# A 1-core network of eight stages: weight splits ahead of use are pinned to ScalarE's program order, and their stores are issued from ScalarE's DMA queue

## The chip, the cores and the metric

The kernel runs on one core of a Trainium2 chip. The metric is the device time of one execution in microseconds. Names used below: TensorE (PE) multiplies, VectorE (DVE) and ScalarE (ACT) work elementwise, GpSimd (POOL) helps them, SyncE (SP) issues DMAs. Each engine runs its own instructions strictly in the order in which they stand.

## What is computed

The reference takes x of 512 rows by 1024 columns in float32 through two blocks of a network. The first block is four residual layers (mixer_a, mixer_b, mixer_c, mixer_a), the second is two layers of a mixer and a gated feed-forward part. Nearly all the work is products of activations with weights. The two kinds that matter here, shortened:

```
def mixer_c(h, w_in, w_grp, scale, w_out):
    proj = h @ w_in                       # 4 groups of xc, then z
    pooled = stack([causal_mean(xc[:, :, g], w) for g, w in enumerate((2, 4, 8, 16))])
    mixed = einsum('bsgc,gcd->bsgd', pooled - xc, w_grp) * scale
    return (mixed * silu(z)) @ w_out

def swiglu(h, w_gate, w_up, w_down):
    return (silu(h @ w_gate) * (h @ w_up)) @ w_down

# first block:  x = x + mixer_a | mixer_b | mixer_c | mixer_a (rms_norm(x))
# second block: x = x + rms_norm(even_mixer | swiglu | odd_mixer | swiglu (rms_norm(x)))
```

## The kernel before

The stages run one after the other and are called a0, b, c, a1 (first block), m0, f0, m1, f1 (second block; m are the mixers, f the feed-forward parts).

**Products in three parts.** A float32 value is held as the sum of a high part (rounded by a Copy on ScalarE) and a low part (value minus high part, a subtraction on VectorE). Each product is three matmuls: high by high, high by low, low by high. A panel of weights (128 x 1024) against 512 rows of activations is therefore 8 x 3 = 24 matmuls of 128x512. `gemm_T` does one panel.

**Weights, the ordinary way.** `wchunk` fetches the raw panel `wr` by a DMA on SP (line 254, in `fetch`), makes `wh` on ScalarE (line 320) and `wl` on VectorE. Each of the three lives in pool `pw` with three buffers, so the preparation can lead TensorE by about two panels. Activations are split likewise into `xh`/`xl`, `mh`/`ml`, `yh`/`yl`.

**Weights, the other way.** The weights of m0, f0's first panels, m1 and f1's first panels are split earlier, in stages with spare time on ScalarE and VectorE, and put back in DRAM as `preh` and `prel`. Their panels are later loaded already split (lines 316, 317, 357 and 358). The generator `presplit` (lines 283 to 311) does this. One step of it loads a raw piece `pr` (line 300, on SP), issues the stores of the piece before (lines 289 and 290), and at its next turn makes `ph` (line 304, ScalarE) and `pl` (VectorE). `pr` has one buffer, `ph` and `pl` have two each. `gemm_T` and its sibling `gemm_tok` give the generator one turn per product (`tick`). The call says how large the pieces are, at every how many turns a piece is made, and how many pieces: 1024 columns, every third, 18 pieces in stage c; 512 columns, every second, in a1; up to 1024 columns, every second, in f0, from its third pair of panels on, beside `ssm_tables`, which builds tables of powers for m1 on VectorE (tiles `E`, `eu`, `btx`). There are 70 pieces: 46 for m0 and f0, and 24 for m1 and f1.

**What sets the order.** A scheduler places the instructions on each engine from the program and from its own model of times, and may hoist an instruction ahead of where the program has it, as early as its operands and buffers allow. An instruction wrapped in `tc.keep_in_program_order` keeps its place among the others of its engine as the program has it. In the kernel before, TensorE and VectorE have such stretches (the class `Ordered`, line 206); ScalarE has none. In the built program of before, the pieces do not stand where the turns of the generator are: all 46 pieces of m0 and f0 stand within stage c, about one ahead of each panel's `wh`, and the 24 of f0 stand in about half of that stage.

**Stage c.** Two halves, each with two pooling groups and an output product. A group has four panels of `c_wx` (each followed by running sums in tiles `pad` and `last`, on VectorE and GpSimd, and the split `mh`/`ml`), four of `c_wz` (then `z` through Silu, line 924), and four panels of 512 columns of `c_wg` against `mh`/`ml`, whose results times `z` are split into `yh`/`yl`. Eight panels of `c_wo` against `yh`/`yl` end the half. At the first of these panels the row norm is turned into a scale: `sc` (VectorE, then line 498 on GpSimd), `t` (a diagonal, VectorE), and a small product `a` of `t` with `ones` on TensorE, which is pinned in TensorE's order ahead of the second half of that panel.

Of the kernel before, what the change touches and what calls it, by code (L numbers as in the profile page):

```python
# [179 lines left out]
def build(nc, tc, A, out, stages=("a0", "b", "c", "a1", "m0", "f0", "m1", "f1")):  # L180
# [6 lines left out]
    AF = mybir.ActivationFunctionType  # L187
# [3 lines left out]
    V, S, G, PE = nc.vector, nc.scalar, nc.gpsimd, nc.tensor  # L191
# [25 lines left out]
    def tl(pool, shape, tag, dt=F32, **kw):  # L217
        uid[0] += 1
        return pool.tile(list(shape), dt, tag=tag, name=f"{tag}_{uid[0]}", **kw)

    with ctx:
# [26 lines left out]
        def f32(t):  # L248
            return t.bitcast(F32)
# [33 lines left out]
        def presplit(pool, cap, every, count):  # L283

            made = []

            def store():
                h, l, wh, wl = made.pop(0)
                nc.sync.dma_start(h, f32(wh))
                nc.sync.dma_start(l, f32(wl))  # L290
            while todo and count:
                w, o = todo.pop(0)
                n = min(cap, w.n - o)
                if o + n < w.n:
                    todo.insert(0, (w, o + n))
                count -= 1
                e = slice(o, o + n)
                wr = tl(pool, (P, cap), "pr")[:, :n]
                wh, wl = (tl(pool, (P, cap), "p" + a, F32R, bufs=2)[:, :n] for a in "hl")
                nc.sync.dma_start(wr, w.src[:, e])  # L300
                if made:
                    store()
                yield
                S.activation(wh, wr, AF.Copy)
                V.tensor_tensor(wl, wr, f32(wh), op=SUB)
                made.append((w.h[:, e], w.l[:, e], wh, wl))
                for _ in range(every - 1):
                    yield
            if made:
                store()  # L310
# [249 lines left out]
        def layer_a(j, nxt):  # L560
            with ExitStack() as c:
# [10 lines left out]
                if todo:  # L572
                    tasks.append(presplit(newpool(c, "pre"), 512, 2, 99))
# [304 lines left out]
        def layer_c(nxt):  # L878
            with ExitStack() as c:
# [9 lines left out]
                if "m0" in stages:  # L889
                    todo.extend((w, 0) for w in m0_weights() + (ffn_first(0) or []))  # L890
                    tasks.append(presplit(newpool(c, "pre"), 1024, 3, 18 if "a1" in stages else 99))
# [782 lines left out]
        def layer_f(l, nxt):  # L1674
            with ExitStack() as c:
# [7 lines left out]
                for part, n in enumerate(FFN_SPLIT):  # L1683
                    Y = []
                    for i in range(i0, i0 + n):
                        if l == 0 and i == 2 and "m1" in stages:
                            todo.extend((w, 0) for w in m1_weights() + (ffn_first(1) or []))
                            tasks.append(presplit(newpool(c, "pre"), 1024, 2, 99))
                            tasks.append(ssm_tables(ptab, Y[-1][0]))
                        pg = first.pop(0) if first else gemm_T(A[f"f{l}_wg"][i], X)  # L1690
                        pu = first.pop(0) if first else gemm_T(A[f"f{l}_wu"][i], X)
                        z = tmp()
                        V.tensor_tensor(z, pg, sb, op=MUL)
                        S.activation(z, z, AF.Silu)
                        V.tensor_tensor(z, z, pu, op=MUL)
                        Y.append(split(py, "y", z))
                    i0 += n
                    if part == len(FFN_SPLIT) - 1:
                        drain()
                        sandwich_end(A[f"f{l}_wd{part}"], Y, O, False, 9 + 2 * l, m1_first() if l == 0 else None, sc)  # L1700
                        break
                    for m in range(KD):
                        ps = gemm_T(A[f"f{l}_wd{part}"][m], Y)
                        if part == 0:
                            V.tensor_copy(O[m], ps)
                        else:
                            V.tensor_tensor(O[m], O[m], ps, op=ADD)
# [43 lines left out]
```

## Time and profile before

| | us |
|---|---|
| three runs | 2947.56, 2938.97, 2943.58 |
| median | 2943.58 |
| the profiled execution | 2942.7 |
| its span in the trace | 2940.9 |
| TensorE busy | 2838.7 (97%) |
| VectorE busy | 1618.5 (55%) |
| ScalarE busy | 1033.9 (35%) |
| GpSimd busy | 212.8 (7%) |

The profiled execution moved 385.48 MB by DMA, and TensorE's mean granted clock in it was 0.983 of full speed. In the trace stage c with the pieces for m0 and f0 fills 940 to 1280 us, a1 goes to about 1680 us, and f0's stretch with the pieces for m1 and f1 is 1945 to 2170 us. A row gives the time that an engine sat idle just before a group of instructions and what ended that wait; on an engine that is not the one that bounds the kernel such idle time costs nothing by itself. Ends of matmuls are modelled, so neighbours overlap by a part of their length.

### The profile page before, as it was taken

How to read it: one execution, taken by the hardware profiler on the slowest of the kernel's cores; microseconds unless marked ns; L12 is line 12 of the kernel's file. 1: busy time of each engine (PE TensorE's matmuls, PEld its weight loads, DVE VectorE, ACT ScalarE, POOL GpSimd, SP SyncE). 2: the span in 40 equal slices, each digit the busy share in tenths (PEclk: the TensorE clock that was granted, in tenths of full speed). 3: DMA queues.
4: the chain of work that ended last, by engine and by line, in shares of the span. 5: the costliest groups of instructions: out<-in, count | busy, mean ns of one | idle time of the engine just before them, and what ended most of it. 6: DMA issues, size and time to landing. Idle time of an engine off the chain costs nothing. (4 is left out here: it accounts for less than half of the span.)

```text
span 2940.9 us, 35039 instructions
## 1 busy us (share of the span) xinstructions
PE 2838.7 (97%) x13542; PEld 2332.4 (79%) x13542; DVE 1618.5 (55%) x3092; ACT 1033.9 (35%) x1661; POOL 212.8 (7%) x187
## 2 busy tenths in 40 slices
PE   8999999999999999899999998889999999999998
PEld 7888888888888777678888886677878865888886
DVE  4454654545556564653554587368753577343434
ACT  4322444444444442342222314443332325332222
POOL 2000000000000101220010100120000200200001
PEclk9999999999999999999999999899999999999999
DMA  4222332222223786642222352257862350333222
GB/s 161 93 86 94 128 112 85 90 76 94 72 95 129 245 281 210 207 153 95 92 93 93 120 188 93 83 181 266 294 221 91 133 178 29 115 108 101 93 99 67
DMA packets 127415, 385.48 MB, mean 131 GB/s; under 512 B 16144, under 2 KB 23056, under 8 KB 127248
## 3 DMA queue, kind: packets, MB, share of 16 engines
q1 hardware_dynamic: 127248, 383.25, 38.7%
q8 instruction: 106, 1.74, 0.2%
q14 instruction: 61, 0.50, 0.1%
HBM read 312.94 MB, written 70.25 MB: 130 GB/s over the span
## 5 line engine op out<-in xcount | busy, mean ns | idle before, releaser
L320 ACT ACTIVATE wh<-wr 128x1024 fp32r<-128x1024 f32 (+2 forms) x408 | 420.6, 1032 | 1005.5 <-PE g L205 781.3
L205 PE MATMUL g<-xh,wl 128*128 128x512 f32 (+1 forms) x1720 | 659.9, 384 | 13.0 <-DVE wl L205 9.6
L205 PE MATMUL g<-xl,wh 128*128 128x512 f32 (+1 forms) x1720 | 661.1, 384 | 11.1 <-DVE xl L205 10.9
L205 PE MATMUL g<-xh,wh 128*128 128x512 f32 (+1 forms) x1720 | 664.8, 387 | 5.8 <-DMA wh<-preh 4.8
L205 DVE TENSOR_TENSOR wl<-wr,wh 128x1024 fp32r<-128x1024 f32 (+2 forms) x408 | 507.7, 1245 | 292.3 <-ACT wh L320 287.2
L205 PE MATMUL g<-yh,wh 128*128 128x512 f32 (+1 forms) x1046 | 394.9, 378 | 1.8 <-ACT yh L438 1.1
L205 PE MATMUL g<-yl,wh 128*128 128x512 f32 (+1 forms) x1046 | 391.2, 374 | 1.6 <-DVE yl L205 1.6
L205 PE MATMUL g<-yh,wl 128*128 128x512 f32 (+1 forms) x1046 | 390.2, 373 | 0.6 <-DVE wl L205 0.6
L205 PEld LDWEIGHTS g<-xh,wl 128*128 128x128 f32 x1720 | 326.3, 190 | 81.1 <-DVE wl L205 15.0
L205 PE MATMUL g<-wh,xh 128*128 128x512 f32 (+1 forms) x992 | 381.3, 385 | 7.8 <-ACT wh L320 7.8
L205 PEld LDWEIGHTS g<-xl,wh 128*128 128x128 f32 x1720 | 326.7, 190 | 75.8 <-DVE xl L205 14.9
L205 PEld LDWEIGHTS g<-xh,wh 128*128 128x128 f32 x1720 | 326.9, 190 | 67.9 <-DMA wh<-preh 5.6
L205 PE MATMUL g<-wl,xh 128*128 128x512 f32 (+1 forms) x992 | 376.5, 380 | 0.3 <-DVE wl L205 0.3
L205 PE MATMUL g<-wh,xl 128*128 128x512 f32 (+1 forms) x992 | 375.2, 378 | 0.0
L470 POOL TENSOR_TENSOR acc<-acc,t 128x256 f32<-128x256 f32 (+1 forms) x109 | 119.6, 1097 | 1708.2 <-issue 1418.3
L205 PEld LDWEIGHTS g<-yh,wh 128*128 128x128 f32 x1046 | 197.6, 189 | 39.4 <-ACT wh L320 2.0
L205 PEld LDWEIGHTS g<-yl,wh 128*128 128x128 f32 x1046 | 197.7, 189 | 38.3 <-DVE yl L205 2.3
L205 PEld LDWEIGHTS g<-yh,wl 128*128 128x128 f32 x1046 | 197.6, 189 | 34.8 <-DVE wl L205 1.0
L205 PEld LDWEIGHTS g<-wh,xh 128*128 128x128 f32 x992 | 187.7, 189 | 41.1 <-ACT wh L320 7.8
L205 PEld LDWEIGHTS g<-wh,xl 128*128 128x128 f32 x992 | 187.6, 189 | 34.3
L205 PEld LDWEIGHTS g<-wl,xh 128*128 128x128 f32 x992 | 187.9, 189 | 33.4 <-DVE wl L205 1.0
L205 DVE TENSOR_TENSOR t<-g,sb 128x512 f32<-128x512 f32 x112 | 77.1, 690 | 234.5 <-PE g L205 233.9
(309 smaller groups left out, 2706.4 us busy)
## 6 DMA issues: line engine op xcount, KB each, us to landing
wh<-preh SPq DMA_DIRECT2D x48, 512.0 KB, 3.6
wl<-prel SPq DMA_DIRECT2D x48, 512.0 KB, 4.3
wr<-in_f_wg_dram SPq DMA_DIRECT2D x40, 512.0 KB, 3.5
wr<-in_f_wu_dram SPq DMA_DIRECT2D x40, 512.0 KB, 3.5
preh<-ph SPq DMA_DIRECT2D x39, 512.0 KB, 5.3
prel<-pl SPq DMA_DIRECT2D x39, 512.0 KB, 6.4
wr<-in_a_wv_dram SPq DMA_DIRECT2D x32, 512.0 KB, 3.5
wr<-in_a_wu_dram SPq DMA_DIRECT2D x32, 512.0 KB, 3.5
```

What stands on the lines that cost most here:

```text
L205: r = f(*a, **k)
L320: S.activation(wh[:, :n], wr[:, :n], AF.Copy)
L470: G.tensor_tensor(self.acc[:, t], self.acc[:, t], sq[:, t], op=ADD)
```

## The change

Two edits in `presplit`. The two stores of each piece are issued from ScalarE's DMA queue and not from SP's. The Copy that makes `ph` is wrapped in `tc.keep_in_program_order`.

```diff
@@ -286,8 +286,8 @@
             def store():
                 h, l, wh, wl = made.pop(0)
-                nc.sync.dma_start(h, f32(wh))
-                nc.sync.dma_start(l, f32(wl))
+                nc.scalar.dma_start(h, f32(wh))
+                nc.scalar.dma_start(l, f32(wl))
...
@@ -301,7 +301,7 @@
                 yield
-                S.activation(wh, wr, AF.Copy)
+                tc.keep_in_program_order(S.activation(wh, wr, AF.Copy))
                 V.tensor_tensor(wl, wr, f32(wh), op=SUB)
```

The built programs show what this moves. ScalarE has 1611 rows for 1471 before (140 stores more), SP 735 for 875; TensorE's order is almost untouched. Of the 46 pieces for m0 and f0, 18 now stand in stage c, one at every third panel, and 28 in a1, at every second product; the 24 of f0 stand at every second panel over most of that stage.

ScalarE in the second group of stage c's first half, at the end of its `c_wx` panels and through its `c_wz` panels (`wh` are panels, `ph` pieces, `mh` the split of the pooled differences):

```order
 L320 ACTIVATE wh_9294<-wr_9296 128x1024
-L304 ACTIVATE ph_11419<-pr_11418 128x512
 L924 ACTIVATE z_9221<-z_9221 128x512
 L320 ACTIVATE wh_9334<-wr_9336 128x512
-L304 ACTIVATE ph_11506<-pr_11505 128x512
+L304 ACTIVATE ph_9326<-pr_9325 128x1024
 L924 ACTIVATE z_9257<-z_9257 128x512
-L304 ACTIVATE ph_11593<-pr_11592 128x512
+L289 DMA preh_1476_7900<-ph_9326 128x1024
+L290 DMA prel_1477_7901<-pl_9327 128x1024
 L320 ACTIVATE wh_9360<-wr_9362 128x512
```

Where three pieces stood within four panels, one stands, right behind a `wh`, with its two stores behind it on the same engine.

VectorE at the opening of stage c, ahead of the norm scale `sc` (`wl` are low parts of panels, `pl` of pieces):

```order
 L205 SCALAR_TENSOR_TENSOR xl_7732<-x_7518,gains_82,xh_7731 128x512
-L205 TENSOR_TENSOR wl_7810<-wr_7811,wh_7809 128x1024
-L205 TENSOR_TENSOR pl_8569<-pr_8567,ph_8568 128x1024
 L205 TENSOR_TENSOR wl_7980<-wr_7981,wh_7979 128x1024
 L205 TENSOR_TENSOR wl_8027<-wr_8028,wh_8026 128x1024
-L205 TENSOR_TENSOR pl_8657<-pr_8655,ph_8656 128x1024
+L205 TENSOR_TENSOR pl_8012<-pr_8010,ph_8011 128x1024
 L205 TENSOR_SCALAR sc_7828<-a_7829 128x4
 L205 TENSOR_SCALAR t_7836<-ident_106,sc_7828 128x128 x4
```

The piece right ahead of `sc` is now the first of the stage and not the seventh or eighth, and the one ahead of it is gone.

VectorE in f0, where the tables of powers are built (`E` and `eu` are steps of a table, `o` a copy of an output product):

```order
-L205 MEMSET E_17398 128x1 x2
+L205 COPY o_15110<-g_16306 128x512
 L205 TENSOR_SCALAR eu_17401<-E_17398,s_3082_15387 128x1
 L205 TENSOR_SCALAR eu_17404<-E_17398,s_3083_15389 128x1
+L205 TENSOR_TENSOR wl_16441<-wr_16442,wh_16440 128x1024
 L205 SCALAR_TENSOR_TENSOR E_17398<-E_17398,s_3083_15389,eu_17401 128x1
```

This table now stands ahead of panel `wl_16441`, which stood well ahead of it before: the tables move forward past panels, and four of the eight fall within ten panels.

## Rows read from the trace of the kernel before

**Rows 1.** Windows of four stretches: length; busy us (instructions) per engine; clock; DMA share; GB/s.

```profile
940.00:1280.00 340.00, 314.27 (x1314) 250.91 (x1313) 204.83 (x283) 131.34 (x176) 48.88 (x32) 0.96 0.71 232
1280.00:1680.00 400.00, 399.74 (x1836) 332.87 (x1835) 192.60 (x226) 118.69 (x162) 35.16 (x23) 1.00 0.30 99
1945.00:2170.00 225.00, 212.93 (x947) 173.76 (x946) 176.87 (x564) 84.68 (x108) 1.90 (x3) 0.98 0.83 281
2170.00:2300.00 130.00, 130.00 (x577) 107.52 (x576) 53.17 (x68) 36.12 (x47) 3.54 (x3) 1.00 0.31 99
```

**Rows 2.** Lines of TensorE, 940 to 1280: count, busy, mean ns, idle before, releaser.

```profile
L205 PE MATMUL g<-xh,wl 128*128 128x512 f32 x256 | 101.8, 398 | 6.0 <-DVE wl L205 6.0
...
L205 PE MATMUL g<-yh,wh 128*128 128x512 f32 x112 | 44.8, 400 | 1.8 <-ACT yh L438 1.1 <-ACT wh L320 0.7
...
L205 PE MATMUL g<-mh,wh 128*128 128x512 f32 x64 | 27.7, 432 | 7.6 <-ACT wh L320 7.6
L205 PE MATMUL g<-mh,wl 128*128 128x512 f32 x64 | 27.5, 430 | 2.6 <-DVE wl L205 2.4
...
L205 PE MATMUL a<-t,ones 128*128 128x128 f32 x8 | 2.1, 441 | 5.5 <-DVE t L205 5.5
```

**Rows 3.** Timeline of ScalarE in the wg panels: start, length, instruction, idle before.

```profile
1191.46 0.63 ACT L304 ACTIVATE ph<-pr 128x512 fp32r<-128x512 f32 x1 [3.40 <-DMA pr<-in_m_wo_dram]
...
1196.77 0.63 ACT L304 ACTIVATE ph<-pr 128x512 fp32r<-128x512 f32 x1 [4.16 <-issue]
1197.31 0.61 ACT L320 ACTIVATE wh<-wr 128x512 fp32r<-128x512 f32 x1
```

**Rows 4.** Lines of ScalarE, line 304: 940 to 1270, then 1945 to 2160.

```profile
L304 ACT ACTIVATE ph<-pr 128x512 fp32r<-128x512 f32 (+1 forms) x46 | 36.7, 798 | 131.8 <-issue 45.7 <-DMA pr<-in_m_wo_dram 31.9 <-DMA pr<-in_m_wqk_dram 21.4
...
L304 ACT ACTIVATE ph<-pr 128x1024 fp32r<-128x1024 f32 (+2 forms) x24 | 24.6, 1024 | 78.0 <-DMA pr<-in_m_wo_dram 15.0 <-DMA pr<-in_m_win_dram 9.7 <-DMA pr<-in_m_wq_dram 9.1
```

**Rows 5.** Timeline of VectorE at the norm scale of stage c, 984 to 994.

```profile
984.85 2.35 DVE L205 TENSOR_TENSOR wl<-wr,wh 128x1024 fp32r<-128x1024 f32 x2
991.43 1.23 DVE L205 TENSOR_TENSOR pl<-pr,ph 128x1024 fp32r<-128x1024 f32 x1 [4.23 <-ACT ph L304]
992.58 0.15 DVE L205 TENSOR_SCALAR sc<-a 128x4 f32<-128x4 f32 x1
993.86 0.88 DVE L205 TENSOR_SCALAR t<-ident,sc 128x128 f32<-128x128 f32 x4 [1.13 <-POOL sc L498]
```

**Rows 6.** Windows of 10 us on TensorE: busy (instructions), clock, DMA share, GB/s.

```profile
990.00:1000.00 10.00, 5.80 (x18) 0.66 0.92 318
1250.00:1260.00 10.00, 9.50 (x37) 0.88 0.46 162
```

**Rows 7.** Lines of TensorE, 1945 to 2170, then of VectorE, 1945 to 2160.

```profile
L205 PE MATMUL g<-xh,wh 128*128 128x512 f32 x230 | 91.1, 396 | 3.5 <-DMA wh<-preh 3.5
...
L205 PE MATMUL g<-xh,wl 128*128 128x512 f32 x229 | 90.6, 396 | 3.6 <-DVE wl L205 3.6
...
L205 PE MATMUL a<-ident,btx 128*128 128x128 f32 x12 | 2.8, 302 | 3.4 <-DVE btx L205 3.4
...
L205 DVE SCALAR_TENSOR_TENSOR E<-E,s,eu 128x1 f32<-128x1 f32 (+5 forms) x144 | 34.6, 271 | 0.3
L205 DVE TENSOR_SCALAR eu<-E,s 128x1 f32<-128x1 f32 (+5 forms) x144 | 30.1, 248 | 1.6
```

**Rows 8.** Timeline of VectorE in the last pooling group, 1234 to 1244.

```profile
1234.62 0.69 DVE L205 SCALAR_TENSOR_TENSOR t<-last,pad 128x512 f32<-128x512 f32 x1 [2.30 <-POOL last L910]
...
1243.21 0.69 DVE L205 SCALAR_TENSOR_TENSOR t<-last,pad 128x512 f32<-128x512 f32 x1 [2.29 <-POOL last L910]
```

**Rows 9.** Tile prel: issue ns min/median/max. Then DMA issues: count, KB, us to landing.

```profile
L290 SPq DMA_DIRECT2D prel<-pl x70: 319/424/1409, 942.7 to 2159.0; - x70
...
preh<-ph SPq DMA_DIRECT2D x39, 512.0 KB, 5.3
prel<-pl SPq DMA_DIRECT2D x39, 512.0 KB, 6.4
```

## The prediction

> **What bounds the kernel now.** The table of busy times is read first: TensorE is busy 2838.7 us of a span of 2940.9, so about 102 us of idle TensorE time and the half-clock time inside the busy part (mean clock 0.983) are all that a change to splits and stores can give back. The windows by stage come next, since an average says nothing on where the 102 us lie [rows 1]. In a1 TensorE is busy 399.74 of 400 us and in the later part of f0 130.00 of 130. That last row gives the price of a matmul at full clock: 130 / 577 = 0.2253 us, so 5.4 us for a panel of 24. In stage c, 1314 matmuls would take 1314 x 0.2253 = 296 us, and they take 340: 44 us are lost, 25.7 as idle time (340 - 314.27), about 13.6 by the clock (4% of 340), the rest at restarts. In f0's stretch with splits 12.1 us are idle and the clock costs 2% of 225 = 4.5.
>
> Third come the releasers of TensorE's idle time in stage c [rows 2]. Nearly all of it is ended by a weight split that came late (`wh` on ScalarE, `wl` on VectorE) or by `t` of the norm scale. None is ended by a DMA. Fourth, why `wh` is late though ScalarE is busy only 131 of 340 us: the timeline of ScalarE [rows 3]. The split `ph` of a piece stands ahead of the panel's `wh`; ScalarE runs in order and sits 3.4 to 4.2 us until the raw piece has come, and only then makes `wh`, at 1197.31. Line 304 takes 131.8 us of idle ScalarE time in this way for 46 pieces, and 78.0 us for the 24 of f0 [rows 4]. The pieces thus go at the pace of their own loop (load, split, store, next load, with one `pr` buffer), and panels that TensorE needs now queue behind pieces that are needed hundreds of microseconds later.
>
> **The change part by part.** The pin puts each piece where the generator's turn is: behind a `wh`, with its raw data fetched a turn or more earlier. A `ph` then costs ScalarE its own length and no wait. The idle times of [rows 2] are taken one by one.
>
> *Norm scale, 5.5 us.* Before `sc`, VectorE makes two `wl` until 987.2, waits 4.2 us for a `ph` and makes its `pl` at 991.43; `sc` follows at 992.58 and `t` at 993.86 [rows 5]. The order now has one piece there, the first of the stage, whose `pr` came long before. Without the wait: 987.2, plus 1.15 for `pl` (991.43 to 992.58), 0.15 for `sc` and 1.13 for GpSimd lets `t` start at 989.6, 4.2 us earlier than at 993.86. So 4.2 of the 5.5 us could go; I take 3.6, since the `pl` may stand a little later behind its `ph`. *The `wg` panels, 7.6 + 2.6 = 10.2 us* [rows 2]: their period is half a panel, 2.7 us, and a `ph` with its wait takes longer than that [rows 3]. Now one piece stands in every three panels and waits for nothing: 9.5 go. *The `yh` panels, 1.8 us, and the small groups* (25.7 - 5.5 - 10.2 - 6.0 - 1.8 = 2.2): 3.5 of 4.0 go, as they too wait for `wh` and `wl`. *The `xh,wl` panels, 6.0 us*: some 3.3 of it lie in the last pooling group, where VectorE's chain waits for GpSimd's running sums every 8.6 us (1234.62 to 1243.21) against 5.4 us for a panel [rows 8]. That chain is the kernel's own and stays. Of the other 2.7, 2.5 go. Together 3.6 + 9.5 + 3.5 + 2.5 = 19 us of idle time.
>
> *The clock.* After long waits the granted clock falls: 0.66 in the 10 us with the norm scale, 0.88 in the last pooling group [rows 6]. Of the 13.6 us in stage c some 3.4 belong to that last group, whose waits stay; 10 go with the waits that go. **Stage c: -29 us**, with -20 as the end where the clock gives little and the other loops stay, and -38 where nearly all of the 44 comes back.
>
> *Pieces moved from c to a1.* 28 splits at 0.63 us on ScalarE and up to 1.2 us on VectorE, their loads and 56 stores now stand in a1. Cover: ScalarE is busy 118.69 of 400 us there, VectorE 192.60, DMA 0.30 [rows 1], and TensorE sees only `wh` and `wl`, which lead by two panels (10.8 us). 18 + 34 us of more work on these two engines leave both under 60%: 0, or +4 where some panel meets a piece with no lead left.
>
> *f0.* Idle before `xh,wl` 3.6 us, before `a<-ident,btx` 3.4, before `xh,wh` 3.5 (the first split panel's own load, in a stretch where DMAs are busy 0.83) [rows 7], and 12.1 - 10.5 = 1.6 in small groups. With half as many pieces per panel and no waits at `ph`: 3.6 + 1.5 + 1.0 + 0.5 = 6.6, plus 2 of the clock's 4.5: -8.6 (from -4 to -13). Against it, the order packs four tables into ten panels. A table costs VectorE (34.6 + 30.1) / 8 = 8.1 us [rows 7]; four of them, ten `wl` and five `pl` at 1.2 us and the copies and products there come to about 55 to 58 us in the 54 us of ten panels: +2 (0 to +4), spread by the lead. **f0: -6.6 us.**
>
> *The stores.* 140 issues leave SP and go to ScalarE. On SP one takes 0.42 us in the median and at most 1.41 [rows 9]. No row shows a store issued by ScalarE, so the price there is bounded: from nothing (a gain is excluded for ScalarE, since it issues no stores now) to the landing of 6.4 us [rows 9] if the issue held the engine until the data is out. I take the SP row's 0.42, since it is the same operation on another queue: 59 us over the whole run, in stretches where ScalarE is idle more than 60% of the time, so 0. The store of `pl` makes ScalarE wait for VectorE; queued behind it are the next `wh` and the next `z` or `yh`. The order puts `pl` right behind a `wl` nearly everywhere, so this wait is a microsecond or two, under the two-panel lead. On SP, panel loads no longer queue behind stores that wait for `ph`, but no TensorE wait in c ends at a load of a raw panel: 0.
>
> The Trainium skill ("DMA: Bandwidth & Descriptors", section "Issuing engines are not separate DMA queues") says that transfers started by different engines share the same 16 DMA engines and that spreading the issues "will only save the time on the sequencer it takes to initiate the DMA". By that rule the queue edit alone gives nothing here, as SP's issue time bounds no panel; the rows above lead to the same 0, and the rule speaks against expecting a gain from the queue, not against the pin.
>
> Sum: -29 + 0 - 6.6 + 0 = -35.6. Against the profiled execution, 2942.7 - 35.6 = **2907 us**. Its time is 0.9 below the median of the runs, which is left aside.
>
> **The rivals.** *Part of the idle time is the kernel's own.* The waits that now end at `wh` would end next at other chains: GpSimd's loop of 8.6 us in the deep pooling groups [rows 8], the norm scale, and VectorE, which is busy 205 of 340 us. Speaking for it: the running-sum loop is there in two groups of four, and VectorE is already the releaser of most of the `xh,wl` and `mh,wl` waits. Against it: the waits at the `wg` panels end at ScalarE, and nothing but the pieces is in front of it. Then c gives 16 and f0 5: 2942.7 - 21 = 2922 us.
>
> *More comes back.* If c runs at full clock but for the last group and f0 loses nothing: 38 + 13 + a few, 2942.7 - 54 = 2889 us.
>
> *The change hardly does what it says.* If the pieces' positions on ScalarE are the new ones but real times let the same loop hold it (a load of `pr` that comes late because its buffer is freed late), the waits move and do not shrink: 2940 us. Against it: two or three panels, 10.8 to 16.2 us, now lie between pieces, and the loop took about 7 us (340 / 46).
>
> *Slower: the stores hold ScalarE.* If each issue on ScalarE occupied it until the data has landed, a pair would take 5.3 + 6.4 = 11.7 us [rows 9]. In f0, with one piece in two panels (10.8 us), ScalarE's other work is (84.68 - 24.6) / 225 x 10.8 = 2.9 us, with the piece's 1.0 it is 3.9 [rows 1, 4], so 15.6 us are needed in 10.8: +4.8 for 24 pieces. In a1 it is 118.69 / 400 x 10.8 = 3.2, plus 0.63 and 11.7, so +4.7 for 28 pieces [rows 1]. Together +115 + 132 = +247: 2907 + 247 = 3154 us. It decides from (10.8 - 3.9) / 2 = 3.4 us per store; the longest issue of a `prel` store on SP took 1.41 [rows 9], which speaks against it.
>
> **How the numbers follow.** Forecast (2890 to 2918): 0.60. Part of the idle time is the kernel's own (2918 to 2930): 0.20. More comes back (under 2890): 0.07. Within 0.3% of the time before, about what a measurement of this kernel can tell from no change (2934 to 2951): 0.06, the case that hardly does what it says. Stores hold ScalarE: 0.07, with smaller holds in it. The range of 2890 to 2930 takes in the forecast and its partial rival, 0.80. Faster is 0.60 + 0.20 + 0.07 = 0.87, same 0.06, slower 0.07.
>
> **What would show it right or wrong.** In the profile of the changed kernel the idle time before line 304 should be near nothing (now 131.8 and 78.0), the waits of TensorE for `wh` in the `mh` groups gone, and the stretch from 940 some 29 us shorter, while a wait of 3 us or so stays in the last pooling group. The clock in the norm scale's 10 us should stand near 0.9. a1 should stay at 400 us with 28 pieces in it. The issues at lines 289 and 290 should read about 0.4 us on ScalarE. It would be wrong if TensorE in a1 showed idle time ended by `wh` or `wl`, if ScalarE's waits before `prel` stores were longer than the two-panel lead, or if f0's table stretch became VectorE's.

## The result and the profile after

The changed kernel takes 2894.24 us in the median (2890.71 to 2899.0, 4 runs) beside 2944.59 us of the kernel before: a ratio of 0.9832, 95% interval 0.9809 to 0.9855. That is faster by 50 us or 1.7%, where 35.6 us were forecast (2907 us); it lies inside the range of 2890 to 2930. The span of the profiled execution is 2888.9 us for 2940.9.

Where the 52 us of span went is read from the start times of the same matmul in both traces. TensorE's matmuls are 13542 in both and stand in nearly the same order, so the n-th of one can be set beside the n-th of the other (n counted from 0; times in us from the start of the span; differences taken before rounding):

| matmul, place | before | after | difference |
|---|---|---|---|
| 4600, ahead of stage c | 915.7 | 916.5 | +0.8 |
| 5000, behind the norm scale of c | 1006.9 | 997.5 | -9.4 |
| 5400, first output product of c | 1107.8 | 1089.0 | -18.8 |
| 5800, where the last pooling group of c begins | 1211.4 | 1179.6 | -31.8 |
| 6400, in a1 | 1356.3 | 1316.7 | -39.7 |
| 8600, in m0 | 1846.0 | 1806.2 | -39.8 |
| 9000, in f0 | 1929.5 | 1889.6 | -39.9 |
| 10000, in f0 behind the tables | 2163.5 | 2112.3 | -51.2 |
| 13400, in f1 | 2907.0 | 2855.1 | -51.8 |

Stage c is 40.4 us shorter (from +0.8 to -39.7), a1 and m0 are unchanged, f0 is 11.4 us shorter, and the rest is under 1 us.

The windows of the same four stretches after the change answer to [rows 1]; the columns are those of that group, and the bounds are moved by the differences above:

```profile
941.00:1241.00 300.00, 297.94 (x1316) 245.12 (x1315) 185.03 (x255) 116.20 (x148) 51.25 (x32) 1.00 0.55 188
1241.00:1641.00 400.00, 399.75 (x1836) 333.12 (x1835) 210.48 (x255) 133.28 (x190) 33.86 (x23) 1.00 0.48 155
1906.00:2119.00 213.00, 208.69 (x945) 172.59 (x946) 172.65 (x560) 80.13 (x104) 1.76 (x2) 1.00 0.74 258
2119.00:2249.00 130.00, 130.00 (x577) 107.55 (x576) 56.90 (x69) 40.25 (x51) 3.81 (x3) 1.00 0.50 164
```

TensorE idles 2.1 of 300 us in stage c, for 25.7 of 340, and the granted clock reads 1.00 in all four. In a1 it is busy 399.75 of 400 us as before, though 28 pieces and their 56 stores now lie there (ScalarE 133.3 us for 118.7, VectorE 210.5 for 192.6, DMA 0.48 for 0.30). In f0 4.3 us are idle, for 12.1.

TensorE's groups in stage c, as in [rows 2] (count, busy, mean ns, idle before, releaser):

```profile
L205 PE MATMUL g<-xh,wl 128*128 128x512 f32 x256 | 99.8, 390 | 0.8 <-DVE wl L205 0.8
...
L205 PE MATMUL g<-mh,wh 128*128 128x512 f32 x64 | 24.9, 389 | 0.0
...
L205 PE MATMUL g<-mh,wl 128*128 128x512 f32 x64 | 24.9, 389 | 0.0
L205 PE MATMUL a<-t,ones 128*128 128x128 f32 x8 | 1.1, 274 | 0.0
```

The 7.6 + 2.6 us at the `wg` panels, the 5.5 at the norm scale and 5.2 of the 6.0 before `xh,wl` are gone. The cause is read on ScalarE, in its group of line 304 over the whole execution, which answers to [rows 4]:

```profile
L304 ACT ACTIVATE ph<-pr 128x1024 fp32r<-128x1024 f32 (+2 forms) x70 | 60.3, 862 | 18.2 <-DMA pr<-in_m_wo_dram 10.4 <-DMA pr<-in_m_wq_dram 2.8 <-DMA pr<-in_s_wg_dram 2.5
```

131.8 + 78.0 us of idle ScalarE time before the pieces have become 18.2. The issues of the store of the low part, now on ScalarE (ns min/median/max), answer to [rows 9]:

```profile
L290 ACTq DMA_DIRECT2D prel<-pl x70: 326/362/363, 985.1 to 2173.1; - x70
```

An issue lasts 0.33 to 0.36 us. The timeline of ScalarE in the third pooling group, the first of the second half, shows one piece from end to end (it is the place of [rows 3] and of the first order listing under "The change"; the text there puts that listing in the first half and in the `c_wx` and `c_wz` panels by mistake: it runs from the last panel of `c_wz` into those of `c_wg`, which are the ones of 512 columns):

```profile
1159.83 0.62 ACT L320 ACTIVATE wh<-wr 128x512 fp32r<-128x512 f32 x1
1160.36 1.04 ACT L304 ACTIVATE ph<-pr 128x1024 fp32r<-128x1024 f32 x1
1161.30 0.61 ACT L924 ACTIVATE z<-z 128x512 f32<-128x512 f32 x1
1161.43 0.33 ACTq L289 DMA_DIRECT2D preh<-ph  x1
1162.76 0.36 ACTq L290 DMA_DIRECT2D prel<-pl  x1
1163.28 0.63 ACT L320 ACTIVATE wh<-wr 128x512 fp32r<-128x512 f32 x1 [1.36 <-PE g L205]
```

The panel's `wh` goes first, the piece follows without any wait, the store issued at 1161.43 lies within the `z` of 1161.30 to 1161.91, both stores are issued within 2.8 us of its start, and the next `wh` is made as soon as TensorE has freed a buffer for it (idle time ended by PE).

### The profile page after: what moved, and what is told of

Read it like the earlier page. It is cut to its first block, busy times and chain, and to the rows that moved or that the text cites. A ratio compares the mean times of both kernels' runs of the same rounds, so it can differ in the third digit from the quotient of the medians.

```text
span 2888.9 us, 35009 instructions
## 1 busy us (share of the span) xinstructions
PE 2814.6 (97%) x13542; PEld 2322.2 (80%) x13542; DVE 1616.3 (56%) x3092; ACT 1033.3 (36%) x1661; POOL 215.0 (7%) x187
## 5 line engine op out<-in xcount | busy, mean ns | idle before, releaser
L205 PE MATMUL g<-xl,wh 128*128 128x512 f32 (+1 forms) x1720 | 657.7, 382 | 13.4 <-DVE xl L205 13.2
```

Of the source, the lines that this page charges most:

```text
L205: r = f(*a, **k)
```

## The experiments

All ratios are against the kernel before, run beside the variant on one chip.

**The pin alone, and the queue alone.** The change has two edits, so each was run by itself.

```diff
-                S.activation(wh, wr, AF.Copy)
+                tc.keep_in_program_order(S.activation(wh, wr, AF.Copy))
```

> The pin alone; the stores stay on SP. Theory (pieces stand on ScalarE ahead of panels and hold them while their raw data is fetched; the queue is worth nothing): the whole gain, 2889 to 2899 us, idle time before line 304 under 30 us in all, stage c about 40 us shorter than before and f0 about 11. Rival (the stores on SP, each waiting for a piece, hold up SP's loads, and the other queue frees them): most of the gain is missing, 2925 us or more.

Measured: 2892.19 us, ratio 0.9834 (0.9819 to 0.985), the whole gain. Stage c is 41.8 us shorter and f0 13.2. Line 304 waits for next to nothing:

```profile
L304 ACT ACTIVATE ph<-pr 128x1024 fp32r<-128x1024 f32 (+2 forms) x70 | 60.2, 861 | 0.7 <-DMA pr<-in_m_win_dram 0.7
```

Run once more beside the changed kernel on one chip, the two differ by 2 us:

> The changed kernel once more, beside the two above on one chip: 2889 to 2900 us. With the pin, the pieces stand where pl follows a wl at once, so ScalarE's waits at the low stores should be short; against the run with the pin alone the queue should be worth nothing within 0.3% either way. A rival in which the queue helps once the pin is there would show over 10 us between the two.

> The pin alone once more, on the same chip as the changed kernel: within 0.3% of it (9 us). Theory: the queue is worth nothing with the pin. Rival: it is worth over 10 us one way or the other.

Measured: 2893.3 us for the changed kernel (0.9839, 0.9826 to 0.9852) and 2895.65 us for the pin alone (0.9848, 0.9835 to 0.986). With the pin, the queue is worth nothing that can be told. Without it the queue costs time:

```diff
-                nc.sync.dma_start(h, f32(wh))
-                nc.sync.dma_start(l, f32(wl))
+                nc.scalar.dma_start(h, f32(wh))
+                nc.scalar.dma_start(l, f32(wl))
```

> The stores alone go to ScalarE's queue; no pin, so the pieces stay ahead of the panels. Theory: no gain, 2935 to 2955 us, or somewhat slower where a store of prel makes ScalarE wait for VectorE ahead of a panel; idle time before line 304 in stage c near the 131.8 us of before. Rival (SP's queue was the brake): 2895 to 2910 us and the idle time before line 304 mostly gone.

Measured: 2960.28 us, ratio 1.0066 (1.0054 to 1.0078). The rival on SP's queue falls: with no store on SP, line 304 still waits for raw data, 117.0 us in stage c and 92.8 in f0's stretch (ScalarE's groups of line 304 in the two stretches):

```profile
L304 ACT ACTIVATE ph<-pr 128x512 fp32r<-128x512 f32 (+1 forms) x45 | 35.6, 791 | 117.0 <-DMA pr<-in_m_wo_dram 34.1 <-DMA pr<-in_m_wqk_dram 24.5 <-DMA pr<-in_m_wab_dram 18.7
...
L304 ACT ACTIVATE ph<-pr 128x1024 fp32r<-128x1024 f32 (+2 forms) x24 | 24.6, 1024 | 92.8 <-DMA pr<-in_m_wo_dram 25.0 <-DMA prel<-pl 13.1 <-DMA pr<-in_m_win_dram 12.7
```

By the matmuls' start times stage c is 3 us shorter than before and f0 22 us longer (from -2.3 at matmul 9000 to +19.8 at 10000). To see which of the two stores costs that, each was moved alone, without the pin:

> The kernel before with only the stores of the high parts (preh) on ScalarE's queue; no pin. They wait for ScalarE's own ph. Theory (what costs time in the run with the queue alone is ScalarE waiting, at a store of a low part, for VectorE's pl, which stands behind a table in f0): no change beyond 0.3%, 2932 to 2950 us. Rival (the issues themselves, 0.33 us each, or the order that they bring, cost it): half of the loss or more, 2950 us and up.

Measured: 2946.73 us, ratio 1.0022 (1.0013 to 1.0032): slower by 0.2%, within the 0.3% that was named. By stages it is less quiet: c 8 us shorter, f0 8 us longer. In f0 that is over a third of the 22 us, though a high store waits for ScalarE's own `ph` alone; there the rival, the issues or the order that they bring, is borne out.

> The kernel before with only the stores of the low parts (prel) on ScalarE's queue; no pin. They wait for VectorE's pl. Theory: all of the loss of the run with the queue alone, 2952 to 2968 us, and it lies in f0's stretch with the tables, where wh comes late. Rival (issues or order): about half, 2945 to 2953 us, or none.

Measured: 2972.96 us, ratio 1.0114 (1.0101 to 1.0128), above the 2952 to 2968 that were named and more than both stores together. So over the whole run the low store is the one that costs, as expected, but not only among the tables: stage c is 12.6 us longer and f0 13.5. ScalarE's timeline in f0 shows how one low store holds it:

```profile
2109.27 1.06 ACT L304 ACTIVATE ph<-pr 128x1024 fp32r<-128x1024 f32 x1 [3.64 <-DMA pr<-in_m_wo_dram]
2111.62 0.36 ACTq L290 DMA_DIRECT2D prel<-pl  x1
2112.11 1.06 ACT L320 ACTIVATE wh<-wr 128x1024 fp32r<-128x1024 f32 x1 [1.77 <-DVE eu L205]
```

`ph` ends at 2110.3, the store is issued at 2111.62 and the `wh` behind it starts at 2112.11, after an idle time of 1.77 us. VectorE's timeline has the `pl` that the store waited for, from 2110.37 to 2111.6:

```profile
2110.37 1.23 DVE L205 TENSOR_TENSOR pl<-pr,ph 128x1024 fp32r<-128x1024 f32 x1 [0.60 <-ACT ph L304]
```

This `pl` began as soon as `ph` was done, so no table stood between them. Each variant also moves other instructions, since the scheduler places anew around the stores, so the share of these waits in the 32 us was not measured by itself. It is not shown that they are its cause: the changed kernel has longer waits of this kind and loses nothing by them, as the next section shows.

**Is it the wait for raw data, or so many pieces?** The kernel before with its pieces as dense as they were, but without their fetch: every piece splits one raw panel that is loaded once per stage, so the split weights are not those of the reference.

```diff
-            made = []
+            made, raw = [], tl(pool, (P, cap), "pr")
+            for c0 in range(0, cap, 512):
+                nc.sync.dma_start(raw[:, c0:c0 + 512], todo[0][0].src[:, :512])
...
-                wr = tl(pool, (P, cap), "pr")[:, :n]
+                wr = raw[:, :n]
...
-                nc.sync.dma_start(wr, w.src[:, e])
```

> The kernel before with the fetch of the pieces left out: every piece splits the same raw panel that is loaded once per stage, so the split weights are not the right ones. The pieces stand as densely as before and ahead of the panels. Theory (the wait for raw data is what ScalarE sits for): stage c loses most of its idle time, 2895 to 2915 us, and line 304 waits for under 40 us in all, mostly for stores to free its buffers. Rival (so many pieces in a row are themselves too much work for ScalarE and VectorE in stage c): 2925 us or more, with TensorE's waits for wh or wl still there.

Measured: 2898.19 us, ratio 0.985 (0.9835 to 0.9866), in the range of the theory. With no pin and all 46 pieces in stage c, the stage is 34 us shorter than before. ScalarE still waits 56.0 us there (95.5 in all, more than the 40 expected), now mostly for stores to free a `ph` buffer:

```profile
L304 ACT ACTIVATE ph<-pr 128x512 fp32r<-128x512 f32 (+1 forms) x46 | 36.5, 797 | 56.0 <-DMA preh<-ph 32.5 <-DVE pl L205 11.4 <-DVE fx L205 4.0
```

TensorE's wait at the `wg` panels is gone (7.6 us before):

```profile
L205 PE MATMUL g<-mh,wh 128*128 128x512 f32 x64 | 24.9, 389 | 0.0
```

So the number of splits and their place ahead of the panels make 6 of the 40 us at most; the fetch makes the rest. This run also takes the traffic of the fetches off the DMA engines. That it is the wait for them and not the traffic is left to the two runs below that fetch the same bytes with one raw buffer and with two.

**A pinned piece at every turn.** The changed kernel with `presplit(newpool(c, "pre"), 1024, 1, 99)` in stage c for `presplit(newpool(c, "pre"), 1024, 3, 18 if "a1" in stages else 99)`.

> The changed kernel with all pieces of m0 and f0 made in stage c, one at every turn and of 1024 columns (32 pieces in the first half of the stage, none in a1): pinned, but as dense as before. Theory (position, not density): stage c gains nearly as much as with the change where a panel takes 5.4 us, but in the wg panels (2.7 us) the fetch of about 3.5 us is longer than a turn and the waits come back: 2895 to 2912 us, of which a1 gives at most 1. Rival (density, that is the move of pieces into a1, is what gives the gain): 2920 us or more.

Measured: 2951.71 us, ratio 1.003 (1.0018 to 1.0043). This was a miss: stage c is not 30 to 40 us shorter than before but 13 longer, in spite of the pin. The timeline of ScalarE says why (three pieces in a row):

```profile
1112.32 1.06 ACT L304 ACTIVATE ph<-pr 128x1024 fp32r<-128x1024 f32 x1 [3.75 <-DMA pr<-in_m_wv_dram]
...
1119.67 1.06 ACT L304 ACTIVATE ph<-pr 128x1024 fp32r<-128x1024 f32 x1 [3.47 <-DMA pr<-in_m_wv_dram]
...
1128.45 1.06 ACT L304 ACTIVATE ph<-pr 128x1024 fp32r<-128x1024 f32 x1 [4.76 <-DMA pr<-in_m_wv_dram]
```

Pieces stand 7.3 to 8.8 us apart, and at each ScalarE waits 3.5 to 4.8 us for raw data. A piece's own loop (fetch, `ph`, `pl`, buffer free) takes some 7.5 us with one raw buffer. Where the turns lie closer together than that, the pinned piece holds ScalarE, and with it all panels, at the loop's pace. The pin is thus not what removes the wait; it keeps the distance that the generator asks for, and that distance has to be longer than the loop. That is a correction to the theory of this run, which had said that a place behind a panel is enough. The prediction had set the distance beside the loop, under its rival that the change hardly does what it says. In the `wg` panels of the changed kernel two pieces stand 8.6 us apart (1171.98 and 1180.57), less than the 10.8 named there but more than the loop, and neither waits. Three runs put it to the test.

> The changed kernel with all pieces of m0 and f0 made in stage c, 32 pieces of 1024 columns, one at every second turn (10.8 us of TensorE work, 5.4 in the wg panels), none in a1. Theory as the run with one piece per turn has left it (a piece costs TensorE nothing if its raw data is there when its turn comes, that is if the turns lie further apart than the piece's own loop of fetch, split and free buffer, some 7 us): nearly all of the gain, 2893 to 2910 us, small waits in the wg panels alone. Rival (moving pieces out of stage c is what gives the gain): 2925 us or more.

Measured with `1024, 2, 99`: 2908.88 us, ratio 0.9885 (0.9867 to 0.9902). Until the end of stage c this kernel gains 35 of the 40 us without moving a single piece to a1, so the move to a1 is not the source. It then gives 9 back: the generator has pieces left over, and ahead of the last output product the pieces that remain are made in one go (`drain`). ScalarE's timeline there:

```profile
1253.26 1.06 ACT L304 ACTIVATE ph<-pr 128x1024 fp32r<-128x1024 f32 x1 [5.02 <-DMA pr<-in_m_wo_dram]
...
1260.57 1.06 ACT L304 ACTIVATE ph<-pr 128x1024 fp32r<-128x1024 f32 x1 [2.16 <-DMA pr<-in_f_wg_dram]
```

and TensorE's at the opening of a1:

```profile
1288.85 0.80 PE L205 MATMUL g<-wh,xh 128*128 128x512 f32 x1 [3.68 <-ACT wh L320]
```

The pieces are 7.3 us apart again, with waits of 5.02 and 2.16 us, and TensorE idles 3.68 us for a `wh`.

> The changed kernel with pieces of 512 columns, one at every turn of stage c (64 pieces) and none in a1, one raw buffer. Theory (the turn is shorter than the piece's loop, so ScalarE sits for raw data at nearly every piece): 2925 to 2960 us, idle time before line 304 over 100 us. Rival (the larger pieces of the run with one piece per turn were too much work per panel): under 2910 us.

> As the run with pieces of 512 columns at every turn, with two raw buffers in stage c in place of one: nothing else differs in the program. Theory (it is the fetch that the pinned piece waits for): the fetch runs a turn further ahead, idle time before line 304 falls to under a third of that run's, and most of the loss is gone, 2890 to 2910 us. Rival (the number of splits per panel on ScalarE and VectorE): no better than with one buffer, within 8 us of it.

The edits are `512, 1, 99` in stage c, and in the second run also `bufs=2` for `pr` there. Measured: 2952.28 us (1.0037, 1.0024 to 1.0051) with one raw buffer and 2914.5 us (0.9904, 0.9888 to 0.9919) with two. ScalarE's group of line 304 from 940 to 1420 us with one buffer:

```profile
L304 ACT ACTIVATE ph<-pr 128x512 fp32r<-128x512 f32 x64 | 40.3, 630 | 123.5 <-DMA pr<-in_m_wo_dram 28.3 <-DMA pr<-in_m_wab_dram 26.8 <-DMA pr<-in_m_wqk_dram 25.5
```

and with two:

```profile
L304 ACT ACTIVATE ph<-pr 128x512 fp32r<-128x512 f32 x64 | 39.9, 623 | 38.0 <-DMA pr<-in_m_wo_dram 12.0 <-DMA pr<-in_f_wu_dram 8.0 <-DMA pr<-in_f_wg_dram 6.0
```

A second raw buffer is worth 38 us at the same number of pieces per turn: the fetch runs a turn ahead, and the wait falls from 123.5 to 38.0 us, under a third. At matmul 5800, ahead of the last pooling group, the run with two buffers is 31.3 us ahead of the kernel before, as far as the changed kernel (31.8) in spite of a piece at every turn; the run with one is 14.9 ahead. The rest of the difference comes behind that, in the last group and in the `drain`. The time with two is 4 us above the range that was named. That lies in the `drain` too, where twelve pieces stand in a row; TensorE's timeline has one wait of 12.76 us there:

```profile
1268.32 0.80 PE L205 MATMUL g<-yh,wh 128*128 128x512 f32 x1 [12.76 <-ACT wh L320]
```

**The last pooling group.** The prediction had left 6.7 us to GpSimd's running sums there. The kernel before with these sums on VectorE:

```diff
-                                (G if sh > 1 else V).tensor_tensor(
+                                V.tensor_tensor(
```

> The kernel before with the running sums of stage c on VectorE in place of GpSimd, which takes 8.6 us per panel out of the loop in the last pooling group. As the prediction had it (that loop is what TensorE waits for in the last group, 3.3 us idle and 3.4 by the clock): 4 to 8 us faster than before. As the trace of the changed kernel suggests (the loop is still there and TensorE does not wait, so the waits of before came from pieces): within 3 us of before or slower, as VectorE has more to do.

Measured: 2932.08 us, ratio 0.996 (0.9945 to 0.9975), 9 us faster, a little above the 4 to 8 of the first expectation and far from the second. Stage c is 12.5 us shorter, and f0, where the edit changes nothing, 4 longer. The `xh,wl` waits of stage c are gone:

```profile
L205 PE MATMUL g<-xh,wl 128*128 128x512 f32 x256 | 100.2, 392 | 0.0
```

while ScalarE's wait before the pieces is as long as before:

```profile
L304 ACT ACTIVATE ph<-pr 128x512 fp32r<-128x512 f32 (+1 forms) x46 | 36.8, 799 | 140.4 <-issue 54.7 <-DMA pr<-in_m_wo_dram 34.8 <-DMA pr<-in_m_wqk_dram 15.8
```

In the changed kernel it is the other way round. Its VectorE still waits for GpSimd in that group, at nearly the old pace (the rows answer to [rows 8], 8.3 us apart for 8.6):

```profile
1191.24 0.69 DVE L205 SCALAR_TENSOR_TENSOR t<-last,pad 128x512 f32<-128x512 f32 x1 [3.41 <-POOL last L910]
...
1199.49 0.69 DVE L205 SCALAR_TENSOR_TENSOR t<-last,pad 128x512 f32<-128x512 f32 x1 [3.41 <-POOL last L910]
```

and TensorE waits only 1.5 us from 1191 to 1222 us. So the waits of before needed both, the loop and the pieces. A reading that fits, though no run tests it: the loop loses some 3 us per panel against TensorE's 5.4, over four panels, which a full lead of two panels (10.8 us) about covers and a lead already spent on pieces does not.

## Why the prediction was right, and where it was off

**The bound and its cause: right.** Pieces that held ScalarE for their raw data made `wh` late; the time came back where the windows had put it, in stage c (-40.4 for -29) and f0 (-11.4 for -6.6). The run without fetches and the two runs with one and two raw buffers show the fetch as the cause. One step was taken without a reason: 45.7 of the 131.8 us stand under "issue" in [rows 4], where the profile names no releaser, and so does the second wait of [rows 3], of 4.16 us. The trace of before bears the step out. The fetch of that piece (SP's timeline, then the tile `pr` from 1192 to 1197.2 us):

```profile
1193.01 0.41 SPq L300 DMA_DIRECT2D pr<-in_m_wo_dram  x1
...
DMA to landing us min/median/max: 3.7/3.7/3.7
```

It landed at 1196.70, and `ph` starts at 1196.77. All 40 pieces of stage c that ScalarE waited for start within 0.1 us of their landing.

**Idle time of stage c: 23.6 us went, 19 were forecast.** At the `wg` panels 10.2 for 9.5, and at `yh` and the small groups 2.7 for 3.5 (4.0 before, 1.3 after). Two terms were too small. At the norm scale all 5.5 went, for 3.6: the working took the end of VectorE's two `wl`, 987.2 in [rows 5], as fixed, but these too had been late behind a piece. They now start at 981.52 for 984.85, and `t` is there before TensorE asks for it:

```profile
981.52 2.36 DVE L205 TENSOR_TENSOR wl<-wr,wh 128x1024 fp32r<-128x1024 f32 x2 [8.31 <-ACT wh L320]
983.80 1.22 DVE L205 TENSOR_TENSOR pl<-pr,ph 128x1024 fp32r<-128x1024 f32 x1
984.94 0.15 DVE L205 TENSOR_SCALAR sc<-a 128x4 f32<-128x4 f32 x1
986.23 0.87 DVE L205 TENSOR_SCALAR t<-ident,sc 128x128 f32<-128x128 f32 x4 [1.13 <-POOL sc L498]
```

At the `xh,wl` panels 5.2 went, for 2.5: the step "That chain is the kernel's own and stays" failed for the last pooling group. The chain stayed, but not TensorE's waits: of the 3 us or so that were to be left in that group, 1.5 are. A loop slower than TensorE was read as a bound, without asking for how many panels it runs and how much lead there is at its start.

**The clock: all 13.6 us of stage c came back, 10 were forecast.** The granted clock fell to its lower level (1.2 GHz) behind the long waits of stage c before [rows 6]; after the change it reads 1.00 over the whole stage, so it stays at the upper one (2.4 GHz). The 3.4 us that were left to the last group went too. The other 3 us of the 40.4 are in what the prediction called restarts, 4.7 of its 44 us, to which its sum gave nothing: 1316 matmuls at 0.2253 us and 2.1 us of idle time make 298.6 of the 300 us now.

**f0: 11.4 us for 6.6.** Idle time fell by 7.8 (6.6 forecast): `xh,wl` 3.6 to 0 and `btx` 3.4 to 2.0, both as forecast, the first split panel's load 3.5 to 1.9 (1.0 was forecast), small groups the rest. The other 3.6 us are about what the clock of 0.98 had cost (it reads 1.00 now); 2 were forecast. The +2 for four tables in ten panels did not come: no `wl` wait is left in the stretch (TensorE's groups, as in [rows 7]):

```profile
L205 PE MATMUL g<-xh,wh 128*128 128x512 f32 x230 | 90.3, 393 | 1.9 <-DMA wh<-preh 1.9
L205 PE MATMUL g<-xl,wh 128*128 128x512 f32 x230 | 89.6, 390 | 0.0
L205 PE MATMUL g<-xh,wl 128*128 128x512 f32 x230 | 89.4, 389 | 0.0
...
L205 PE MATMUL a<-ident,btx 128*128 128x128 f32 x12 | 2.5, 278 | 2.0 <-DVE btx L205 1.9
```

**a1 and the stores: right in the sum, wrong in one size.** 0 forecast, 0 measured for both. The rival in which a store holds ScalarE until it lands falls, at 0.33 to 0.36 us per issue and 3.4 us as its deciding point. The wait of a low store for VectorE, put at "a microsecond or two", is longer where a table stands ahead of the `pl`. ScalarE of the changed kernel in f0:

```profile
2017.61 1.06 ACT L304 ACTIVATE ph<-pr 128x1024 fp32r<-128x1024 f32 x1 [0.36 <-DMA pr<-in_m_wq_dram]
2018.70 0.33 ACTq L289 DMA_DIRECT2D preh<-ph  x1
2024.21 0.36 ACTq L290 DMA_DIRECT2D prel<-pl  x1
2024.67 1.06 ACT L320 ACTIVATE wh<-wr 128x1024 fp32r<-128x1024 f32 x1 [6.00 <-DVE E L205]
```

The next `wh` comes after 6.00 us of idle time, and TensorE is busy all the while (window of TensorE):

```profile
2010.00:2050.00 40.00, 40.00 (x180) 1.00 0.70 240
```

The lead covered it, as the prediction had said it would. So such a wait does not by itself explain why the queue alone costs 0.7% and the low store alone 1.1%; that stays open. The Trainium skill ("DMA: Bandwidth & Descriptors", section "Issuing engines are not separate DMA queues") grants a second issuing engine no more than the sequencer's time. The trace agrees that nothing is gained; that the queue alone comes out at a loss is beyond what the rule says.

**The partial rival (2922 us)** was given 0.20 on the strength of the same reading of the GpSimd loop and fell with it. The time of the case "more comes back" (2889) lay nearer to the result than the forecast's.

What stays open: how much of the loss with the queue alone, and with the low store alone, is ScalarE's wait and how much the issues and the new placement around them, and why the low store alone loses more than both stores moved.

## What to carry to other kernels

Work ahead of use that shares an in-order engine with urgent work must not reach that engine before its data is there. Space its turns wider than its own loop of fetch, work and free buffer, or give the fetch another buffer; pinning the order only keeps the spacing, and with too close a spacing it ties the urgent work to the loop. A store issued from a compute engine takes that engine's time for the wait for its source, so put it where the source is already made, or where a full lead covers the wait, as it did here. When a slow side loop is found beside a stall, count its laps and the lead at its start before calling it a bound.

## What the hardware showed that was not expected

A DMA issue on ScalarE took 0.33 to 0.36 us in the changed kernel, with hardly any spread and in part while the engine was still at an activation, while the same issue on SP took 0.42 us in the median and up to 1.41 us before [rows 9]. And a compute engine that issues a store pays not the transfer, which lands 6.7 us later in the median, but the wait for the store's source, up to 6 us of idle time in the changed kernel.
